# Output projection by seven block products instead of eight, in a hybrid pooling and attention block

## The chip, the cores and the metric

The kernel runs on one core of one Trainium2 chip. The metric is device microseconds of one execution; several executions are timed, and one more is recorded by the hardware profiler. TensorE is the matmul engine, VectorE and ScalarE do the elementwise work, GpSimd a part of it, and SyncE (SP) and ScalarE issue the DMA transfers.

## The reference

The block maps 1024 tokens of 1024 channels (with 16 meta tokens ahead of them). A normalised input is projected into branches; a pooling branch and an attention branch give `y_pool` and `y_attn` (512 channels each), and both are projected up, gated, merged and projected out:

```python
merged = (sigmoid(g_pool) * einsum('blc,cd->bld', y_pool, w_up_pool)
          + sigmoid(g_attn) * einsum('blc,cd->bld', y_attn, w_up_attn))
h = x + einsum('bld,de->ble', merged, w_out)          # 1024 x 1024 by 1024 x 1024
out = rmsnorm(h, final_norm_g)
```

Everything is float32. The change touches the last three lines.

## The kernel before

A float32 product is made of three matmuls of a reduced type: each operand is split into a high part (a copy, on ScalarE) and a low part (the difference, on VectorE or GpSimd), and high x high, high x low and low x high are summed in PSUM (`g_mm3`, `o_mm`). TensorE's instructions stand in the order of the program. The other engines' instructions and the DMA issues are put in order by a scheduler at compile time: each engine takes what its model holds ready, earlier lines of the program first; on the chip each engine then works its list off in that order.

The program ends in these stages. (1) Attention, with the projections of the gates between its steps; the gates are spilled to DRAM. (2) `pooled` for four groups, `attn_gate` and `attn_out` for four pairs of heads. `attn_out` loads the softmax denominators (`rc`), scales Y and splits it. (3) Sixteen up projections, `up(j, a)`: channel block j of 128, pooling (a = 0) or attention (a = 1). Each takes 24 matmuls of 512 columns; `up_weights` loads its weights (`rawu`, two buffers), splits them (`whu`, `wlu`) and reloads the gate (`rl`). In `up(j, 1)` the sum of both branches is split into `gh` (ScalarE) and `gl` (GpSimd). They stand in the order (0,0), (1,0), (2,0), (0,1), (3,0), (1,1) and so on. (4) `wo_chunk` loads the output weights in eight chunks through the same two buffers and splits them. (5) The output: eight tiles of 128 rows, two halves of 512 columns, 24 matmuls each; the last half is cut into two of 256 columns in two banks of PSUM. `out_tile` adds the residual, squares and sums, takes the power on GpSimd, scales and stores. The first three tiles are run in two passes over the weights' chunks.

The PSUM banks of (3) and (5) are taken in turn from two pools of three (`bank`). Tile pools hand out a fixed number of buffers per tag: 8 of tag "b" (gates and `rc`), 8 of tag "y", 13 of tag "g", and 16 of `hq`, which takes the place of the normalised input when the last input projection is done (`HX.close`).

Of the kernel before, what the change touches and what calls it, by code (L numbers as in the profile page):

```python
# [8 lines left out]
F32 = mybir.dt.float32  # L9
# [5 lines left out]
D = 1024  # L15
# [38 lines left out]
def tile_hybrid_block(ctx, tc, x, meta, norm_g, w_in, b_forget, pool_w, pool_scale,  # L54
# [76 lines left out]
    def w_chunk(col, **kw):  # L131
# [573 lines left out]
    def pool_mm(zp, g, plh, pll):  # L705
        yh = btile("yh", F32R, "y")
        yl = btile("yl", F32R, "y")
        for c0, c1 in HALVES:
            ps = bank()
            run(g_mm3(ps, [(pwh[:, g], pwl[:, g], plh[:, c0:c1], pll[:, c0:c1])]))  # L710
            nc.vector.scalar_tensor_tensor(zp[:, c0:c1], ps, psc[:, g:g + 1], zp[:, c0:c1], op0=ALU.mult, op1=ALU.mult)
            nc.scalar.activation(yh[:, c0:c1], zp[:, c0:c1], AF.Copy)
            yls.append(nc.gpsimd.tensor_tensor(yl[:, c0:c1], zp[:, c0:c1], r32(yh[:, c0:c1]), op=ALU.subtract))
        ypl[g] = (yh, yl)

    def attn_in(p):
# [2 lines left out]
        Y[p] = y  # L719

    def attn_gate(p, zs):
        ins = nc.gpsimd.tensor_tensor(Y[p], Y[p], zs, op=ALU.mult)
        if p > 1:
            after(ins, yls[-1])

    def attn_out(p):
        rc = btile("rc")
# [63 lines left out]
    def up(j, a, ws):  # L791
        y = (ypl, ya)[a]
        wh, wl, sg_ = ws
        after(nc.scalar.activation(sg_, sg_, AF.Sigmoid), evacs[-1])
        if a:
            gh = gp.tile([128, SEQ], F32R, name="gh", tag="g")
            gl = gp.tile([128, SEQ], F32R, name="gl", tag="g") if j < 5 else btile("gl", F32R)
            mg.append((gh, gl))
# [55 lines left out]
    run(left[3])  # L854
    attn_gate(2, za[2])
    HX.close()
    hq = ctx.enter_context(tc.tile_pool(name="hq", bufs=16, side="right", reuse_waits="tile"))
    attn_gate(3, za[3])
    second_up = up_weights(1, 0)

    wo = {}

    def wo_chunk(k):
        raw = wp.tile([128, D], F32, name="rawo", tag="raw")
        nc.sync.dma_start(raw, wout[:, k, :])
        hi = hq.tile([128, D], F32R, name="woh", tag="h")
        lo = hq.tile([128, D], F32R, name="wol", tag="h")
        nc.scalar.activation(hi, raw, AF.Copy)
        nc.vector.tensor_tensor(lo, raw, r32(hi), op=ALU.subtract)
        wo[k] = (hi, lo)  # L870

    up(0, 0, first_up)
    for p in range(4):
        attn_out(p)
    up(1, 0, second_up)
    for j in range(8):
        if j < 6:
            up(j + 2, 0, up_weights(j + 2, 0))
        up(j, 1, up_weights(j, 1))
        if j in (2, 3, 4, 5):  # L880
            wo_chunk(j - 2)
    for k in range(4, 8):
# [11 lines left out]
    def out_tile(i, parts):
        r = slice(i * 128, (i + 1) * 128)
        xr = btile("xr", F32, "y")
        sq = btile("sq", F32, "y")
        nc.sync.dma_start(xr, x2[r, :])
        ss = sm.tile([128, 4], F32, name="sso")
        tot = sm.tile([128, 1], F32, name="sst")  # L900
        for n, (ps, c0, c1) in enumerate(parts):
            if ps is None:
                ps = bank()
                o_mm(ps, i, c0, c1, range(KO))
            nc.vector.tensor_tensor(xr[:, c0:c1], ps[:, :c1 - c0], xr[:, c0:c1], op=ALU.add)
            nc.scalar.activation(sq[:, c0:c1], xr[:, c0:c1], AF.Square, scale=D ** -0.5, accum_out=ss[:, n:n + 1])
            if n == 0:
                nc.gpsimd.tensor_scalar(tot, ss[:, :1], EPS, None, op0=ALU.add)
            else:
                nc.gpsimd.tensor_tensor(tot, tot, ss[:, n:n + 1], op=ALU.add)  # L910
            nc.vector.tensor_tensor(xr[:, c0:c1], xr[:, c0:c1], fgb[:, c0:c1], op=ALU.mult)
        nc.gpsimd.tensor_tensor(tot, tot, epsp, op=ALU.pow)
        (a0, a1), (b0, b1) = HALVES
        nc.vector.tensor_scalar(sq[:, a0:a1], xr[:, a0:a1], tot, None, op0=ALU.mult)
        nc.sync.dma_start(o2[r, a0:a1], sq[:, a0:a1])
        nc.scalar.activation(sq[:, b0:b1], xr[:, b0:b1], AF.Copy, scale=tot)
        nc.scalar.dma_start(o2[r, b0:b1], sq[:, b0:b1])
# [12 lines left out]

_INS = ['x', 'meta_tokens', 'norm_g', 'w_in', 'b_forget', 'pool_w', 'pool_scale',
# [25 lines left out]
```

## Time and profile before

| | |
|---|---|
| median of 3 runs | 760.97 us (758.75 to 761.46) |
| profiled execution | 758.1 us |
| its span | 756.4 us |
| TensorE busy | 744.6 us, 98% |
| VectorE, ScalarE, GpSimd busy | 489.0, 370.4, 307.8 us |
| output stage (first to last matmul) | 660.6 to 750.1 us |

The span is what the profiler's rows cover; the execution's own time lies 1.7 us above it. Busy shares are over the whole span, so a stage has to be read in its own window. TensorE's rows are pipelined: each lasts longer than the distance to the next start, and the distance is what counts.

### The profile page before, as it was taken

The numbers are of one execution on the slowest core, as the hardware profiler recorded it, in microseconds if no ns is written. First come the engines' busy times: TensorE is split into PE (matmuls) and PEld (weight loads), VectorE is DVE, ScalarE is ACT, GpSimd is POOL, SyncE is SP. The second block draws the span as 40 slices with busy tenths as digits, with TensorE's granted clock in tenths as the row PEclk, the third lists the DMA queues.
The fourth block names the chain that finished last, engine by engine and source line by source line (L and its number), as shares of the span: only waits on it lengthen the run. The fifth ranks groups of instructions, "written<-read, shape, count | busy, mean of one in ns | idle before, by whom it ended". The sixth has DMA issues, their size and how long they took to land.

```text
span 756.4 us, 10583 instructions
## 1 busy us (share of the span) xinstructions
PE 744.6 (98%) x3746; PEld 633.6 (84%) x3746; DVE 489.0 (65%) x935; ACT 370.4 (49%) x708; POOL 307.8 (41%) x338
## 2 busy tenths in 40 slices
PE   8999999999999999999999999999999999999996
PEld 5997999998898898898988888888888788888885
DVE  4753667768779787698697766891566555534322
ACT  6662456446557555575565445531745553313112
POOL 4331336446416544544364354453573123213111
PEclk9999999999999999999999999999999999999999
DMA  9201132221221222221223322349447663523231
GB/s 312 71 20 38 29 94 75 72 85 50 78 61 45 80 63 70 83 60 50 74 66 105 98 74 78 91 149 339 136 168 208 236 196 102 177 84 132 91 112 55
DMA packets 78151, 79.54 MB, mean 105 GB/s; under 512 B 9857, under 2 KB 61057, under 8 KB 78098
## 3 DMA queue, kind: packets, MB, share of 16 engines
q1 hardware_dynamic: 73344, 63.65, 27.6%
q10 hardware_dynamic: 4754, 15.21, 5.9%
q8 instruction: 29, 0.48, 0.3%
q14 instruction: 24, 0.20, 0.1%
HBM read 57.68 MB, written 21.17 MB: 104 GB/s over the span
## 4 chain that ended last, share of the span: by engine, by line
PE 90%; DVE 3%; issue 1%; ACT 0%; POOLq 0%; POOL 0%; DVEq 0%; ACTq 0%
PE pj L139 67%; PE pj L891 12%; PE po L610 5%; PE ps L550 3%; PE ps L549 2%; PE pj L463 1%; PE pj L256 0%; DVE rl L803 0%; DVE yal L735 0%; DVE S L589 0%; DVE y L731 0%; DVE m L565 0%; ACT S L558 0%; DVE ka L243 0%; DVE xt L176 0%
## 5 line engine op out<-in xcount | busy, mean ns | idle before, releaser
L128 POOL TENSOR_TENSOR wlo<-raw,whi 128x256 fp32r<-128x256 f32 x148 | 121.8, 853 | 199.2 <-ACT whi L126 103.9
L139 PE MATMUL pj<-hh,whi 128*128 128x512 f32 (+4 forms) x768 | 178.9, 361 | 0.2 <-DVE V L262 0.2
L139 PE MATMUL pj<-hl,whi 128*128 128x512 f32 (+4 forms) x768 | 177.1, 359 | 0.0
L139 PE MATMUL pj<-hh,wlo 128*128 128x512 f32 (+4 forms) x768 | 174.7, 359 | 0.0
L139 PEld LDWEIGHTS pj<-hh,wlo 128*128 128x128 f32 x768 | 132.4, 188 | 18.2
L139 PEld LDWEIGHTS pj<-hh,whi 128*128 128x128 f32 x768 | 132.2, 189 | 18.0 <-PE pj L256 0.4
L139 PEld LDWEIGHTS pj<-hl,whi 128*128 128x128 f32 x768 | 131.6, 188 | 17.7
L594 DVE TENSOR_TENSOR pl<-S,ph 128x512 fp32r<-128x512 f32 (+4 forms) x112 | 86.8, 790 | 18.8 <-ACT ph L593 18.2
L602 POOL TENSOR_TENSOR acc<-acc,S 128x272 f32<-128x272 f32 (+4 forms) x80 | 76.4, 955 | 9.8 <-ACT S L590 4.7
L558 ACT ACTIVATE S<-ps,negc 128x400 f32<-128x400 f32 (+2 forms) x96 | 49.3, 515 | 45.1 <-DVE S L556 35.8
L590 ACT ACTIVATE S<-S 128x512 f32<-128x512 f32 (+4 forms) x112 | 49.5, 478 | 32.2 <-DVE S L589 32.0
L593 ACT ACTIVATE ph<-S 128x512 fp32r<-128x512 f32 (+4 forms) x112 | 52.2, 480 | 15.8 <-PE po L610 14.5
L565 DVE TENSOR_TENSOR m<-m,S 128x272 f32<-128x272 f32 (+4 forms) x80 | 41.4, 518 | 23.9 <-ACT S L558 22.2
L294 ACT ACTIVATE st<-pj 128x512 f32<-128x512 f32 x48 | 28.5, 594 | 50.9 <-PE pj L139 28.9
L589 DVE TENSOR_TENSOR S<-S,pt 128x512 f32<-128x512 f32 (+4 forms) x112 | 51.9, 498 | 0.8
L891 PE MATMUL pj<-woh,gl 128*128 128x512 f32 (+1 forms) x136 | 51.9, 382 | 0.0
L891 PE MATMUL pj<-wol,gh 128*128 128x512 f32 (+1 forms) x136 | 51.9, 381 | 0.0
L891 PE MATMUL pj<-woh,gh 128*128 128x512 f32 (+1 forms) x136 | 51.7, 380 | 0.0
L126 ACT ACTIVATE whi<-raw 128x1024 fp32r<-128x1024 f32 x37 | 39.1, 1056 | 25.1 <-PE pj L139 23.3
L807 POOL TENSOR_TENSOR gl<-rl,gh 128x512 fp32r<-128x512 f32 x16 | 22.3, 1396 | 70.9 <-ACT gh L806 70.9
L803 DVE TENSOR_TENSOR rl<-pj,rl 128x512 f32<-128x512 f32 x32 | 22.0, 689 | 31.3 <-PE pj L139 28.0
L556 DVE SCALAR_TENSOR_TENSOR S<-ps,negc,mask 128x128 f32<-128x128 f32 (+2 forms) x72 | 23.7, 330 | 23.0 <-PE ps L550 22.2
(165 smaller groups left out, 1107.4 us busy)
## 6 DMA issues: line engine op xcount, KB each, us to landing
raw<-in_w_in_dram SPq DMA_DIRECT2D x40, 512.0 KB, 3.9
sp_gp<-st SPq DMA_DIRECT2D x16, 256.0 KB, 2.0
sp_ga<-st SPq DMA_DIRECT2D x16, 256.0 KB, 2.0
rl<-sp_gp ACTq DMA_DIRECT2D x8, 512.0 KB, 4.7
rl<-sp_ga ACTq DMA_DIRECT2D x8, 512.0 KB, 4.3
rawo<-in_w_out_dram SPq DMA_DIRECT2D x8, 512.0 KB, 4.2
xr<-in_x_dram SPq DMA_DIRECT2D x8, 512.0 KB, 4.1
xt<-in_x_dram SPq DMA_DIRECT2D x7, 512.0 KB, 7.7
```

The source lines that it names most:

```text
L126: nc.scalar.activation(hi, raw, AF.Copy)
L128: nc.gpsimd.tensor_tensor(lo[:, k:k + 2], raw[:, k:k + 2], r32(hi[:, k:k + 2]), op=ALU.subtract)
L139: nc.tensor.matmul(ps, a, b, start=(i == 0), stop=(i == len(seq) - 1))
L558: nc.scalar.activation(s[:kb, f0:], ps[:kb, f0:], AF.Identity, bias=nb_)
L565: nc.vector.tensor_tensor(m[:kb, c0:], m[:kb, c0:], s[:kb, c0:], op=ALU.max)
L589: nc.vector.tensor_tensor(s[:kb, c0:], s[:kb, c0:], self.pm[:kb, c0:], op=ALU.subtract)
L590: exps.append(nc.scalar.activation(s[:kb, c0:], s[:kb, c0:], AF.Exp))
L593: nc.scalar.activation(ph[:kb, c0:], s[:kb, c0:], AF.Copy)
L594: dves.append(nc.vector.tensor_tensor(pl[:kb, c0:], s[:kb, c0:], r32(ph[:kb, c0:]), op=ALU.subtract))
L602: nc.gpsimd.tensor_tensor(acc[:kb, c0:], acc[:kb, c0:], s[:kb, c0:], op=ALU.add)
L610: nc.tensor.matmul(self.po[:, c0:], v, r[:kb, c0:], start=(b == 0 and i == 0), stop=(b == self.nb - 1 and i == 1))
L891: nc.tensor.matmul(ps[:, :c1 - c0], mg[k][a][:, r], wo[k][b][:, c0:c1], start=(k == 0 and n == 0), stop=(k == KO - 1 and n == 2))
```

## The change

The output product is made by a scheme of Strassen's kind (the form with seven products and fifteen additions): merged and w_out are cut into four blocks of 512 x 512 each. With A the merged activations and B the weights:

S1 = A21 + A22, S2 = S1 - A11, S3 = A11 - A21, S4 = A12 - S2; T1 = B12 - B11, T2 = B22 - T1, T3 = B22 - B12, and B21 - T2.
P1 = A11 B11, P6 = S2 T2, P2 = A12 B21, P7 = S3 T3, P5 = S1 T1, P4 = A22 (B21 - T2), P3 = S4 B22, run in this order.
The output blocks are C11 = P1 + P2, C12 = P1 + P6 + P5 + P3, C21 = P1 + P6 + P7 + P4, C22 = P1 + P6 + P7 + P5.

Each product has four tiles of 128 rows and 12 matmuls a tile, and its operands are split as before, one product ahead (`prep`), into two sets of buffers in turn. Sums that follow each other stay in PSUM (P2 on P1, P7 and P4 on P6, P3 on P5); the other additions go into the residual tiles `xr`. The additions of blocks run on GpSimd (S3, S4 and all T) and VectorE (S1, S2). The merged activations are kept unsplit (`G`), the weights are loaded whole into eight buffers. The pooling up projections 0 to 3 stand ahead of the first one of attention, and weights are asked for one projection ahead. GpSimd's two-input passes (`pool_tt`, `attn_gate`) are cut into pieces of 256 columns.

```diff
+    def pool_tt(out, x, y, op):
+        for c in range(0, out.shape[-1], 256):
+            ins = nc.gpsimd.tensor_tensor(out[:, c:c + 256], x[:, c:c + 256], y[:, c:c + 256], op=op)
+        return ins
...
-        for k in range(0, KO, 2):
-            nc.gpsimd.tensor_tensor(lo[:, k:k + 2], raw[:, k:k + 2], r32(hi[:, k:k + 2]), op=ALU.subtract)
+        pool_tt(flat(lo), flat(raw), flat(r32(hi)), ALU.subtract)
...
     def attn_gate(p, zs):
-        ins = nc.gpsimd.tensor_tensor(Y[p], Y[p], zs, op=ALU.mult)
...
+        for c in range(0, SEQ, 256):
+            ins = nc.gpsimd.tensor_tensor(Y[p][:, c:c + 256], Y[p][:, c:c + 256], zs[:, c:c + 256], op=ALU.mult)
...
             if a:
-                nc.vector.tensor_tensor(sg_[:, c0:c1], sg_[:, c0:c1], gt[j][:, c0:c1], op=ALU.add)
-                nc.scalar.activation(gh[:, c0:c1], sg_[:, c0:c1], AF.Copy)
-                nc.gpsimd.tensor_tensor(gl[:, c0:c1], sg_[:, c0:c1], r32(gh[:, c0:c1]), op=ALU.subtract)
+                nc.vector.tensor_tensor(G[j][:, c0:c1], sg_[:, c0:c1], gt[j][:, c0:c1], op=ALU.add)
...
+    hq = ctx.enter_context(tc.tile_pool(name="hq", bufs=8, side="right", reuse_waits="tile"))
...
+    def w_load(k):
+        W[k] = hq.tile([128, D], F32, name="W", tag="w")
+        nc.sync.dma_start(W[k], wout[:, k, :])
...
+    def split_op(op_, k, src):
+        h_ = pick(op_, k, 0)
+        nc.scalar.activation(h_, src, AF.Copy)
+        nc.vector.tensor_tensor(pick(op_, k, 1), src, r32(h_), op=ALU.subtract)
...
+    def t_first(k):
+        tt(Y3[k // 2][:, k % 2, :], side(W, k, "22"), side(W, k, "12"), ALU.subtract, nc.gpsimd)
+        tt(side(W, k, "12"), side(W, k, "12"), side(W, k, "11"), ALU.subtract, nc.gpsimd)
+    def t_second(k):
+        tt(side(W, k, "11"), side(W, k, "22"), side(W, k, "12"), ALU.subtract, nc.gpsimd)
+    def t_third(k):
+        tt(side(W, k, "21"), side(W, k, "21"), side(W, k, "11"), ALU.subtract, nc.gpsimd)
+    def s_first(k):
+        tt(X3[k // 2][:, k % 2, :], side(G, k, "11"), side(G, k, "21"), ALU.subtract, nc.gpsimd)
+    def s_second(k):
+        tt(side(G, k, "21"), side(G, k, "21"), side(G, k, "22"), ALU.add, nc.vector)
+        tt(side(G, k, "11"), side(G, k, "21"), side(G, k, "11"), ALU.subtract, nc.vector)
+    def s_third(k):
+        tt(side(G, k, "12"), side(G, k, "12"), side(G, k, "11"), ALU.subtract, nc.gpsimd)
...
+    steps = [(2, 0), (3, 0), (0, 1)]
+    for j in range(1, 8):
+        steps += [(j + 3, 0), (j, 1)] if j < 5 else [(j, 1)]
+    ws = {steps[0]: up_weights(*steps[0])}
     for p in range(4):
         attn_out(p)
     up(1, 0, second_up)
+    for n, s in enumerate(steps):
+        if n + 1 < len(steps):
+            ws[steps[n + 1]] = up_weights(*steps[n + 1])
+        up(*s, ws.pop(s))
+        if n < 8:
+            w_load((0, 4, 1, 5, 2, 6, 3, 7)[n])
+            if n % 2:
+                t_first(n // 2)
+        j, a = s
+        if a and j < 4:
+            s_first(j)
+        if s == (7, 0):
+            opA, opB = operand("y"), operand("y")
+        if a and j >= 4:
+            if j < 6:
+                for k in (2 * j - 8, 2 * j - 7):
+                    split_op(opA, k, side(G, k, "11"))
+                    split_op(opB, k, side(W, k, "11"))
+                    t_second(k)
+            if j == 5:
+                s_second(0)
+            if j > 4:
+                s_second(j - 4)
...
+    def prod(ps, A_, B_, i, start, c0=0, c1=512):
+        n = 0
+        for p, q in ((0, 0), (0, 1), (1, 0)):
+            for k in range(4):
+                nc.tensor.matmul(ps[:, c0:c1], pick(A_, k, p)[:, i * 128:(i + 1) * 128], pick(B_, k, q)[:, c0:c1],
+                                 start=start and n == 0, stop=n == 11, skip_group_check=True)
+                n += 1
...
+    def prep(n):
+        A_, B_ = operand("yh"[n % 2]), operand("yh"[n % 2])
+        sa, sb = srcs[n]
+        for k in range(4):
+            split_op(A_, k, side(G, k, sa) if sa else X3[k // 2][:, k % 2, :])
+            split_op(B_, k, side(W, k, sb) if sb else Y3[k // 2][:, k % 2, :])
+            if n == 2:
+                s_third(k)
+                t_third(k)
+        ops[n] = A_, B_
+    for n in range(7):
+        if n < 6:
+            prep(n + 1)
+        ps = bb_ if n in (1, 3, 5) else ba
+        for i in range(4):
+            if n == 6 and i == 3:
+                for c0, c1 in ((0, 256), (256, 512)):
+                    prod(ps[i], *ops[n], i, False, c0, c1)
+                    arrive(i, 512 + c0, ps[i][:, c0:c1])
+                    gain(i, 512 + c0, 512 + c1)
+                store(i, True)
+                continue
+            prod(ps[i], *ops[n], i, n in (0, 1, 4))
             if n == 0:
+                x1 = X1[i // 2][:, i % 2, :]
+                nc.scalar.activation(x1, ps[i], AF.Copy)
+                for r, c in ((i, 1), (i + 4, 1), (i + 4, 0)):
+                    tt(xr[r][:, T_[c]], xr[r][:, T_[c]], x1, ALU.add, nc.gpsimd)
+            elif n == 1:
+                nc.vector.tensor_tensor(xr[i][:, T_[1]], ps[i], xr[i][:, T_[1]], op=ALU.add)
+            elif n == 2:
+                arrive(i, 0, ps[i])
+                if i == 3:
+                    gain(i, 0, 512)
+            elif n == 3:
+                nc.vector.tensor_tensor(xr[i + 4][:, T_[1]], ps[i], xr[i + 4][:, T_[1]], op=ALU.add)
+            elif n == 4:
+                arrive(i + 4, 512, ps[i])
+            elif n == 5:
+                arrive(i + 4, 0, ps[i])
+                store(i + 4)
             else:
+                arrive(i, 512, ps[i])
+                store(i)
```

`arrive` adds a block from PSUM into `xr` (VectorE), squares it (ScalarE) and adds its sum on GpSimd; `gain` multiplies by the norm's gain; `store` takes the power on GpSimd, scales the row (one VectorE pass of 1024 columns with the gain; for the last row two halves, on VectorE and ScalarE) and stores it.

## Rows read from the trace of the kernel before

**Rows 1.** The page: busy time of each engine, and the granted clock in 40 slices.
```profile
PE 744.6 (98%) x3746; PEld 633.6 (84%) x3746; DVE 489.0 (65%) x935; ACT 370.4 (49%) x708; POOL 307.8 (41%) x338
...
PEclk9999999999999999999999999999999999999999
```
**Rows 2.** Windows: length, busy us (instructions) per engine, granted clock, DMA share, GB/s.
```profile
569.50:586.40 16.90, 16.90 (x74) 13.60 (x73) 12.96 (x13) 9.49 (x11) 4.73 (x2) 1.00 0.83 233
...
638.00:660.60 22.60, 22.60 (x98) 18.27 (x98) 12.37 (x17) 8.08 (x12) 7.96 (x6) 1.00 0.48 164
660.60:750.10 89.50, 89.48 (x409) 73.29 (x407) 32.29 (x47) 21.31 (x45) 17.84 (x25) 1.00 0.28 94
```
**Rows 3.** The chain that ended last: start us, us, what.
```profile
589.66 71.13 PE pj L139 x304
```
**Rows 4.** Timeline of TensorE in the output stage: start us, us, instructions.
```profile
660.62 0.39 PE L891 MATMUL pj<-woh,gh 128*128 128x512 f32 x1
...
744.24 0.28 PE L891 MATMUL pj<-woh,gh 128*128 128x256 f32 x1
...
749.80 0.28 PE L891 MATMUL pj<-woh,gl 128*128 128x256 f32 x1
```
**Rows 5.** Timeline at up(0,1): TensorE, its weight loads, VectorE; idle and releaser in brackets.
```profile
586.59 1.11 PE L139 MATMUL pj<-yah,whu 128*128 128x512 f32 x4
...
587.18 1.23 DVE L735 TENSOR_TENSOR yal<-y,yah 128x1024 fp32r<-128x1024 f32 x1
...
589.66 0.76 PEld L139 LDWEIGHTS pj<-yah,wlu 128*128 128x128 f32 x4 [1.01 <-DVE wlu L787]
...
590.70 1.10 PE L139 MATMUL pj<-yah,whu 128*128 128x512 f32 x4
```
**Rows 6.** Timeline of SP's queue, and GB/s in forty slices of 560 to 757 us.
```profile
571.28 4.95 SPq L730 DMA_DIRECT2D rc<-recs  x8
577.13 0.39 SPq L783 DMA_DIRECT2D rawu<-in_w_up_attn_dram  x1
...
642.69 0.65 SPq L898 DMA_DIRECT2D xr<-in_x_dram  x1
...
GB/s 53 0 169 250 297 107 375 152 348 137 226 98 298 107 106 106 114 307 210 120 42 222 60 0 0 56 162 208 218 0 210 3 109 104 36 180 0 106 0 106
```
**Rows 7.** Groups by line and shape, 560 to 757 us: busy us, mean ns, idle.
```profile
L806 ACT ACTIVATE gh<-rl 128x512 fp32r<-128x512 f32 x16 | 10.0, 630 | 25.3 <-DVE rl L805 25.3
L905 DVE TENSOR_TENSOR xr<-pj,xr 128x512 f32<-128x512 f32 x15 | 10.4, 691 | 34.4 <-PE pj L891 30.0 <-DMA out_dram<-sq 4.4
```
**Rows 8.** Single lines: duration ns min/median/max, first and last start, shapes.
```profile
L128 POOL TENSOR_TENSOR wlo<-raw,whi x148: 729/743/1731, 51.3 to 545.5; 128x256 fp32r<-128x256 f32 x148
L722 POOL TENSOR_TENSOR y<-y,rl x4: 2395/2634/3400, 546.2 to 571.4; 128x1024 f32<-128x1024 f32 x4
L807 POOL TENSOR_TENSOR gl<-rl,gh x16: 1286/1302/2093, 593.1 to 666.2; 128x512 fp32r<-128x512 f32 x16
L754 DVE SCALAR_TENSOR_TENSOR u<-s,u x4: 1226/1648/2203, 506.1 to 553.1; 128x1024 f32<-128x1024 f32 x4
L787 DVE TENSOR_TENSOR wlu<-rawu,whu x16: 681/682/1867, 555.6 to 650.3; 128x512 fp32r<-128x512 f32 x16
L803 DVE TENSOR_TENSOR rl<-pj,rl x32: 676/692/693, 573.3 to 662.0; 128x512 f32<-128x512 f32 x32
L805 DVE TENSOR_TENSOR rl<-rl x16: 678/691/1741, 591.6 to 663.2; 128x512 f32<-128x512 f32 x16
```
**Rows 9.** Timeline of VectorE and GpSimd where a 512-column pass meets 256-column pieces.
```profile
484.66 1.13 DVE L594 TENSOR_TENSOR pl<-S,ph 128x512 fp32r<-128x512 f32 x1
...
484.49 2.61 POOL L128 TENSOR_TENSOR wlo<-raw,whi 128x256 fp32r<-128x256 f32 x3
```
**Rows 10.** Timeline of the tail: the last addition and the last issue.
```profile
750.12 0.42 DVE L905 TENSOR_TENSOR xr<-pj,xr 128x256 f32<-128x256 f32 x1 [1.40 <-PE pj L891]
...
753.02 0.34 ACTq L917 DMA_DIRECT2D out_dram<-sq  x1
```

More of the change, by code (lines that the diff above doesn't have):

```diff
@@ L795, in up @@
         if a:
[L796 to L798 removed]
+            G[j] = gp.tile([128, SEQ], F32, name="G", tag="g")
         for c0, c1 in HALVES:
@@ L856, in tile_hybrid_block @@
     HX.close()
-    hq = ctx.enter_context(tc.tile_pool(name="hq", bufs=16, side="right", reuse_waits="tile"))
+    hq = ctx.enter_context(tc.tile_pool(name="hq", bufs=8, side="right", reuse_waits="tile"))
     attn_gate(3, za[3])
     second_up = up_weights(1, 0)
[L861 to L870, printed above, removed]
+    W = {}
@@ new lines, in tile_hybrid_block, with tt, operand @@
+    T_ = (slice(0, 512), slice(512, 1024))
+    def w_load(k):
+        W[k] = hq.tile([128, D], F32, name="W", tag="w")
+        nc.sync.dma_start(W[k], wout[:, k, :])
+    def tt(out, x, y, op, eng):
+        if eng is nc.gpsimd:
+            pool_tt(out, x, y, op)
+        else:
+            eng.tensor_tensor(out, x, y, op=op)
+    def operand(tag):
+        return [[(bp if tag == "y" else hq).tile([128, 2, 512], F32R, name="op" + tag, tag=tag, bufs=8) for _ in range(2)]
+                for _ in range(2)]
@@ new lines, in pick, with side @@
+    def pick(op_, k, n):
+        return op_[n][k // 2][:, k % 2, :]
+    def split_op(op_, k, src):
+        h_ = pick(op_, k, 0)
+        nc.scalar.activation(h_, src, AF.Copy)
+        nc.vector.tensor_tensor(pick(op_, k, 1), src, r32(h_), op=ALU.subtract)
+    X3 = [gp.tile([128, 2, 512], F32, name="X3", tag="g") for _ in range(2)]
+    Y3 = [gp.tile([128, 2, 512], F32, name="Y3", tag="g") for _ in range(2)]
+    def side(d, k, blk):
+        r, c = {"11": (0, 0), "12": (0, 1), "21": (1, 0), "22": (1, 1)}[blk]
+        return d[k + 4 * r][:, T_[c]] if d is W else d[k + 4 * c][:, T_[r]]
@@ L894, in out_tile @@
[L894 to L906, printed above, removed]
-            if n == 0:
-                nc.gpsimd.tensor_scalar(tot, ss[:, :1], EPS, None, op0=ALU.add)
-            else:
[L910 to L917, printed above, removed]
@@ new lines, in tile_hybrid_block @@
+    fgb = gp.tile([128, D], F32, name="fgb", tag="g")
+    nc.scalar.dma_start(fgb, bass.AP(tensor=final_g.tensor, offset=final_g.offset, ap=[[0, 128], [1, D]]))
+    xr = {}
+    for r in (0, 4, 1, 5, 2, 6, 3, 7):
+        xr[r] = btile("xr")
+        nc.sync.dma_start(xr[r], x2[r * 128:(r + 1) * 128, :])
+    bk = [pool.tile([128, 512], F32, name=n) for pool, n in
+          ((pj, "pj"), (pj, "pj"), (pj, "pj"), (psT, "pt"), (p8, "pj"), (p8, "pj"), (p8, "pj"), (psT, "pt"))]
+    ba, bb_ = bk[:4], bk[4:]
@@ new lines, in tile_hybrid_block, with gain @@
+    X1 = [wp.tile([128, 2, 512], F32, name="X1", tag="raw") for _ in range(2)]
+    sss, tots, cnts = {}, {}, {}
+    def prod(ps, A_, B_, i, start, c0=0, c1=512):
[5 more added lines that the diff above has]
+                n += 1
+    def gain(r, c0, c1):
+        nc.vector.tensor_tensor(xr[r][:, c0:c1], xr[r][:, c0:c1], fgb[:, c0:c1], op=ALU.mult)
@@ new lines, in arrive @@
+    def arrive(r, c0, ps):
+        w = ps.shape[-1]
+        part = xr[r][:, c0:c0 + w]
+        nc.vector.tensor_tensor(part, ps, part, op=ALU.add)
+        if r not in cnts:
+            sss[r] = sm.tile([128, 4], F32, name="sso", bufs=8)
+            tots[r] = sm.tile([128, 1], F32, name="sst", bufs=8)
+            cnts[r] = 0
+        n = cnts[r]
+        cnts[r] += 1
+        sq = stg.tile([128, 512], F32, name="sq", tag="st")
+        nc.scalar.activation(sq[:, :w], part, AF.Square, scale=D ** -0.5, accum_out=sss[r][:, n:n + 1])
+        if n == 0:
+            nc.gpsimd.tensor_scalar(tots[r], sss[r][:, :1], EPS, None, op0=ALU.add)
+        else:
+            nc.gpsimd.tensor_tensor(tots[r], tots[r], sss[r][:, n:n + 1], op=ALU.add)
@@ new lines, in store @@
+    def store(r, last=False):
+        o, t = wp.tile([128, D], F32, name="o", tag=("wh", "wl")[r % 2]), tots[r]
+        rr = slice(r * 128, (r + 1) * 128)
+        nc.gpsimd.tensor_tensor(t, t, epsp, op=ALU.pow)
+        (a0, a1), (b0, b1) = HALVES
+        if last:
+            nc.vector.tensor_scalar(o[:, a0:a1], xr[r][:, a0:a1], t, None, op0=ALU.mult)
+            nc.sync.dma_start(o2[rr, a0:a1], o[:, a0:a1])
+            nc.scalar.activation(o[:, b0:b1], xr[r][:, b0:b1], AF.Copy, scale=t)
+            nc.scalar.dma_start(o2[rr, b0:b1], o[:, b0:b1])
+        else:
+            nc.vector.scalar_tensor_tensor(o, xr[r], t, fgb, op0=ALU.mult, op1=ALU.mult)
+            nc.sync.dma_start(o2[rr, :], o)
```

38 lines of the change are left out of this document (9 added, 29 removed).

## The prediction

> **What bounds the kernel now.** I read the page's busy times first: TensorE is busy 98% of the span and its granted clock is at the top (the 2.4 GHz level) in all forty slices [rows 1]. So a saving counts only if it takes matmuls away, and a cost only if it makes TensorE wait. The windows then show where the change falls: the up projections from 569.5 us, the output projection from 660.6 to 750.1 us with TensorE busy 89.48 of 89.50 us [rows 2]. The chain of waits says the same: from 589.66 us it is matmuls back to back [rows 3]. The reader is to see that VectorE, ScalarE and GpSimd have room in the output stage before, so that nobody but TensorE sets its length; the question is whether that stays so.
>
> **What the change removes.** Output matmuls before: fifteen 512-column blocks of 24, so 360, and 48 of 256 columns in the last block. From the first start at 660.62 to the first narrow one at 744.24 us is 83.62 us for 360, 0.2323 us each; the 48 narrow ones fill 744.24 to 750.08, 0.122 us each [rows 4]. After: seven products of four row tiles of 12 are 336, of which the last tile is cut in two, so 324 wide and 24 narrow: 324 x 0.2323 + 24 x 0.122 = 78.2 us for 89.5 before. **Term 1: -11.3 us.**
>
> Before, up(0,1) waits for the attention rows. Its twelve first matmuls run from 586.59 to 590.70 us, 4.11 us for 12 x 0.2323 = 2.79; the weight loads name the last product of attn_out and wlu as releasers [rows 5]. With the pool projections 2 and 3 ahead of it, up(0,1) comes one projection later (24 x 0.2323 = 5.6 us, so at 592.2), while the last yal ends at 587.18 + 1.23 = 588.4. **Term 2: -1.3 us**, with 3.8 us of slack.
>
> **What it adds on the loading side.** The eight W loads (0.5 MB each) no longer wait for two shared buffers: their eight buffers come free with the last projection, near 569.5 us. The queue of SP there holds the eight rc loads (571.28 to 576.23), which attn_out waits for, and then the weights of the next projections at 577.13 [rows 6]. DMA is already at a share of 0.83 between 569.5 and 586.4 us [rows 2]. All eight W in front of rc would move 4.19 MB at the highest rate of a slice here, 375 GB/s [rows 6], so rc and the weights behind it would be 11.2 us late, 7.4 after the slack. None in front costs nothing. The rc loads stand ahead of W in the program and are ready when the last spill store has left, so I take few in front. **Term 3: +1.0 us** (0 to 7.4).
>
> **What it adds on VectorE and GpSimd.** The products take no plain operands; each needs eight halves of 512 columns split into high and low (ScalarE 0.63 us, VectorE 0.69 us each [rows 7, 8]). ScalarE has 8 x 0.63 = 5.0 us of this in a product of 48 x 0.2323 = 11.15 us, plus four copies or squares (2.5 us): hidden. VectorE has 8 x 0.69 = 5.5 us, plus four additions from PSUM at 0.69 [rows 7]: 8.3 of 11.15, hidden too, unless GpSimd is in the way. And it is: a VectorE pass with both inputs in SBUF takes 0.69 alone and up to 1.74 us while GpSimd runs (L805), whereas the pass with one input from PSUM never takes more than 0.693 (L803) [rows 8]. One such meeting with 256-column GpSimd pieces: the 512-column pass takes 1.13 us instead of its 0.68, between pieces that then take 0.87 on average instead of 0.743 [rows 8, 9]. So they take turns, and each turn costs VectorE 0.45 us. The pieces of 256 columns thus hold it less than the 512-column ones before (1.302 us, and L787 at up to 1.87 [rows 8]).
>
> GpSimd's new pieces: 32 in the up stage (t_first 16, s_first 8, t_second 8, for sixteen 1.302 us passes removed) and 40 from the first product on (24 additions of P1, 16 for s_third and t_third). The 40 take 40 x 0.743 = 30 us alone and some 40 x 1.2 = 48 taking turns, so GpSimd is there until product 3 or 4. In such a product VectorE needs 8 x 1.13 + 4 x 0.69 = 11.8 us, 0.65 more than TensorE: 0.65 x 3 to 5 products = 2.0 to 3.3 us if nothing is in reserve.
>
> The reserve is decided in the last four up projections, 4 x 5.57 = 22.3 us of TensorE. VectorE has there 4 x (4 x 0.69 + 0.68) = 13.8 us of the old work, eight splits at 0.68 for product 0 and six of the s_second additions at 0.69, together 23.3, and with t_second's eight turns up to 26.9. So it enters product 0 between 1.0 and 4.6 us late. In product 0 it has the last half's 1.4, s_second(3)'s 1.4 and eight splits at 1.13: 11.8. The low halves are first read by the fifth to eighth matmul of product 1, so 11.15 + 1.6 = 12.75 us is due: TensorE waits 0.1 to 3.7 us. All bounds: 0 (VectorE finds gaps earlier) to 3.7 + 3.3 = 7.0. What is late next is each following prep, since its buffers come free only with the product before. I take the lower middle, since the due time of 1.6 us is granted again at every product. **Term 4: +2.5 us** (0 to 7.0).
>
> The Trainium skill (GPSIMD Engine Reference, Engine selection) speaks against this change: it gives elementwise passes to VectorE and calls GpSimd about half as fast for two inputs. By the rows a 512-column pass costs VectorE 0.69 us if it does it itself, and 2 x 0.45 = 0.9 if GpSimd does it against a VectorE that is always at such a pass [rows 8, 9]. By the rule the 40 pieces would thus be 20 x 0.69 = 13.8 us on VectorE in place of at most 18, and the sum of term 4 at its upper end some 4 us smaller; by the rows the pieces that meet a PSUM pass or an idle VectorE are free, and the chosen value stands.
>
> GpSimd's own changes ahead of this (yl in 2 x 0.743 for 1.302, gates in 4 x 0.743 for 2.634 us [rows 8]) add 0.2 to 0.35 us each, under 3 us in all. What covers them is GpSimd's idle time: it is busy 4.73 of the 16.9 us from 569.5 on [rows 2]; without that cover up(0,0) would start up to 3 us later. The pieces of split_w keep their size. Nothing.
>
> **The tail.** Before, the last matmul is followed by addition, square, the sums and power on GpSimd, scaling and store, from 750.1 to 756.4 us, 6.3 us [rows 10]. After, the same chain, with two differences. Both halves of the last tile lie in one bank, so the second half's matmuls may wait until VectorE has read the first: 0 to 0.9 us (the 0.42 us read [rows 10] and the hops around it, doubled); I take 0.5. And row 2's store, a two-input pass of 1024 columns, 1.23 us alone (L754's shortest, [rows 8]), is ready at about the time of the last addition, since rows end 2.8 us apart and no longer 11: 0 to 1.8 us, I take 0.7. **Term 5: +1.2 us** (0 to 2.7). The Trainium skill (PSUM — Partial Sum Buffer, PSUM bank collisions raise a hardware error) wants accesses of two engines to one bank kept apart by a semaphore; no run here shows it, and by it the 0.5 is paid in full.
>
> **The sum.** -11.3 - 1.3 + 1.0 + 2.5 + 1.2 = -7.9 us. The profiled execution takes 758.1 us (span 756.4), so 750.2; the runs shown have their median 2.9 us above it at 760.97, which I carry along: **753.0 us**.
>
> **Rivals.**
> *VectorE becomes the bound.* Term 4 at its upper end, 7.0: -12.6 + 1.0 + 7.0 + 1.2 = -3.4, so 757.6 us. For it: VectorE's counted work is over TensorE's in the last four projections and in products 0 to 3. Against: VectorE was idle for 10.2 of the last 22.6 us of the up stage before [rows 2], and gaps earlier in the stage can take splits.
> *The W loads run ahead.* Term 3 at 7.4: -12.6 + 7.4 + 2.5 + 1.2 = -1.5, 759.5 us. For it: nothing but the order of issue holds them, and before, SP issued the first xr load at 642.69 us, well ahead of its use [rows 6]. Against: rc is ahead in the program.
> *Slower: GpSimd wins two turns for each of VectorE's.* Place: the splits of products 1 to 4. A split then takes about 1.87 us as L787's longest [rows 8]; 8 x 1.87 + 2.8 = 17.7, 6.6 us over the product, four times 26. -12.6 + 1.0 + 1.2 + 26 = +15.6, 776.6 us. It decides from the point where four products lose 12.6 us, a split of 1.44 us. For it: such long passes occur. Against: those rows met GpSimd passes of 512 columns and more, and the row with 256 shows 1.13.
>
> **How the numbers follow.** Forecast 0.66; VectorE the bound 0.14; W ahead 0.10; two turns for one 0.10. Half a per cent, 3.8 us, is about what this kernel's measurement can tell from no change: faster is below 757.2, slower above 764.8 us. The forecast with terms 3 to 5 between low and middling values reaches from 748.4 (terms 1 and 2 alone with almost nothing lost) to about 757; nearly all of it is faster. VectorE the bound falls on both sides of 757.2, mostly within; W ahead is within. Faster 0.68, same 0.22, slower 0.10. The range takes in the two middle rivals and leaves out the last and the ends: 748 to 760.
>
> **What would show it.** Right: the output stage in 78 to 82 us with the matmuls 0.232 apart; no weight load of up(0,1) waiting; split passes on VectorE of 1.1 us while GpSimd has pieces and 0.69 later; TensorE's waits, if any, at the starts of products 1 to 4, released by VectorE's low halves. Wrong: splits of 1.4 us and more; weight loads between 580 and 600 us waiting for a DMA of weights or for rc; a wait at each product's start up to the last; a tail over 9 us.

## The result, and the profile after

The changed kernel takes 761.45 us (median of 20 runs, 759.68 to 763.53), the kernel before 759.81 us in the same comparison: a ratio of 1.002 (95% interval 1.0011 to 1.0029). The forecast was 753.0 us, 0.989 of the runs shown then, with a range of 748 to 760; the change does not gain, and loses about one and a half microseconds. The profiled execution takes 763.1 us, its span is 760.9 us.

The page of the kernel after, the lines that answer to [rows 1]:
```profile
PE 738.3 (97%) x3686; PEld 628.7 (83%) x3686; DVE 534.0 (70%) x985; ACT 378.9 (50%) x737; POOL 353.4 (46%) x414
...
PEclk9999999999999999999999999999999999999996
```
The 60 matmuls that the change takes away are gone (3746 to 3686), and TensorE is busy 6.3 us less, in a span that is 4.5 us longer. So it waits more. Where it waits is read from windows that are cut at the same places of the program: the stage of the gates and pooled rows, the up projections, the output, the tail. First the kernel before (columns as in [rows 2]):
```profile
500.49:569.49 69.00, 69.00 (x301) 56.05 (x300) 35.67 (x32) 30.18 (x39) 35.35 (x27) 1.00 0.61 209
569.49:660.39 90.90, 90.14 (x385) 72.14 (x384) 54.69 (x72) 43.06 (x55) 23.70 (x16) 1.00 0.60 191
660.39:749.67 89.28, 89.28 (x408) 73.28 (x407) 32.50 (x47) 21.52 (x45) 17.84 (x25) 1.00 0.28 95
749.67:756.40 6.73, 0.41 (x4) 0.20 (x2) 1.34 (x3) 1.23 (x3) 0.93 (x2) 0.90 0.20 78
```
The same four windows of the kernel after, and two short ones, around the ends of TensorE's two long waits (it resumes at 559.29 and at 751.51 us):
```profile
501.96:574.64 72.68, 70.86 (x302) 57.13 (x300) 33.38 (x32) 30.09 (x39) 41.23 (x46) 0.98 0.62 212
574.64:666.87 92.23, 90.10 (x386) 71.88 (x384) 62.06 (x83) 36.02 (x47) 31.42 (x35) 1.00 0.65 211
666.87:753.81 86.94, 78.51 (x349) 64.53 (x347) 69.45 (x86) 37.21 (x82) 50.29 (x63) 0.96 0.16 62
753.81:760.90 7.09, 0.62 (x3) 0.33 (x2) 1.34 (x3) 1.23 (x3) 0.91 (x2) 0.50 0.20 74
...
557.00:564.00 7.00, 5.18 (x17) 3.77 (x16) 2.27 (x3) 4.82 (x7) 5.60 (x8) 0.76 0.67 222
...
752.00:755.00 3.00, 2.44 (x12) 2.14 (x11) 0.85 (x2) 0.07 (x2) 0.43 (x1) 0.50 0.41 168
```
Read the lengths against each other: 3.7 us lost before the up projections, 1.3 us in them, 2.3 us won in the output, 0.4 us lost in the tail, so 3.0 us lost. The other 1.5 us of the spans' difference lies before 500 us, where both programs do the same work: in this execution the granted clock is 0.50 from 47.6 to 51.0 us, where it is 1.00 in the kernel before. These windows are of one execution each; over all runs the medians lie only 1.6 us apart. In the output TensorE is busy 78.51 of 86.94 us where it had no gap before. Of the 8.43 us that are missing 7.79 are one wait. Timelines of the kernel after near the end, one engine at a time (start us, us, engine, line, operation, count, idle and releaser):
```profile
738.41 0.68 DVE L975 TENSOR_TENSOR xr<-pt,xr 128x512 f32<-128x512 f32 x1
740.85 1.28 DVE L1000 SCALAR_TENSOR_TENSOR o<-xr,sst,fgb 128x1024 f32<-128x1024 f32 x1 [1.75 <-POOL sst L992]
742.05 0.68 DVE L975 TENSOR_TENSOR xr<-pj,xr 128x512 f32<-128x512 f32 x1
744.48 1.28 DVE L1000 SCALAR_TENSOR_TENSOR o<-xr,sst,fgb 128x1024 f32<-128x1024 f32 x1 [1.75 <-POOL sst L992]
745.68 1.28 DVE L975 TENSOR_TENSOR xr<-pj,xr 128x512 f32<-128x512 f32 x2
748.11 1.28 DVE L1000 SCALAR_TENSOR_TENSOR o<-xr,sst,fgb 128x1024 f32<-128x1024 f32 x1 [1.15 <-POOL sst L992]
749.84 1.28 DVE L1000 SCALAR_TENSOR_TENSOR o<-xr,sst,fgb 128x1024 f32<-128x1024 f32 x1 [0.44 <-POOL sst L992]
751.04 0.41 DVE L975 TENSOR_TENSOR xr<-pt,xr 128x256 f32<-128x256 f32 x1
...
739.19 0.64 ACT L983 ACTIVATE sq<-xr 128x512 f32<-128x512 f32 x1 [2.91 <-DVE xr L975]
...
740.26 0.55 POOL L992 TENSOR_TENSOR sst<-sst,epsp 128x1 f32<-128x1 f32 x1
...
751.51 2.93 PE L965 MATMUL pt<-opy 128*128 128x256 f32 x12 [7.79 <-DVE xr L975]
```
VectorE's list goes add (L975), scale (L1000), add, scale. A scale waits for its own row's square on ScalarE and power on GpSimd, 1.75 us with VectorE standing still in the steady part, and the next row's addition stands behind it. From 738.41 to 742.05 us that is 3.64 us a row, where TensorE delivers a row every 2.73 us (a product takes 10.93 us for four). VectorE falls behind row by row. The last tile's second half shares a bank with its first, whose read stands at the end of this queue, at 751.04 us; TensorE, done with the first half at 743.7 us, waits 7.79 us for it, and its last twelve matmuls take 2.93 us at the lower clock level, where the twelve of the first half took 1.59.

The wait before the up projections, on ScalarE, GpSimd and TensorE:
```profile
551.37 7.17 ACTq L698 DMA_DIRECT2D rl<-sp_gp  x2
...
547.51 6.92 POOL L731 TENSOR_TENSOR y<-y,rl 128x256 f32<-128x256 f32 x7
554.38 3.80 POOL L120 TENSOR_TENSOR yl<-rl,yh 128x256 fp32r<-128x256 f32 x4
558.15 0.71 POOL L731 TENSOR_TENSOR y<-y,rl 128x256 f32<-128x256 f32 x1
...
558.64 0.60 ACT L301 ACTIVATE st<-pj 128x512 f32<-128x512 f32 x1 [10.02 <-POOL yl L120]
558.89 0.33 ACTq L698 DMA_DIRECT2D rl<-sp_gp  x1
...
554.07 2.02 PE L146 MATMUL pj<-hh,wlo 128*128 128x512 f32 x8
...
559.29 3.52 PE L146 MATMUL pj<-hh,whi 128*128 128x512 f32 x8 [1.82 <-ACT st L301]
```
The kernel before at the same place, where a gate is one pass:
```profile
546.25 5.75 POOL L722 TENSOR_TENSOR y<-y,rl 128x1024 f32<-128x1024 f32 x2
...
548.69 3.67 ACTq L691 DMA_DIRECT2D rl<-sp_gp  x2
```
There the second of two reload issues ends at 552.36 us, right behind the second gate, which ends at 552.00. After the change, of the eight pieces that two gates now are, GpSimd runs seven, then four pieces of yl, then the eighth. The second reload issue ends only at 558.54 us, right behind the last piece of yl, which ends at 558.18 and is the releaser that the row names. The eighth piece, which ends at 558.86, lets the third reload go at 558.89. So ScalarE stands at the second issue until the yl pieces are through, and with it stands the evacuation (L301, the pass that reads a PSUM bank out) whose bank TensorE needs. Which buffer each reload goes into the rows do not name; that the yl pieces free the second one because the last gate piece now comes behind them is argued. The wait itself is 1.82 us; the eight matmuls after it take 3.52 us where eight took 2.02 before, and their window shows the clock at 0.76.

In the up projections TensorE waits until 593.50 us, 1.67 us, for whu of up(3,0), the high part of its weights, and then 0.46 us for wlu, the low part. (The expectations below count the waits of the weight loads at the same places, 2.1 and 0.9 us.) VectorE, ScalarE and TensorE there:
```profile
589.07 0.69 DVE L810 TENSOR_TENSOR rl<-pj,rl 128x512 f32<-128x512 f32 x1 [1.89 <-PE pj L146]
589.68 1.22 DVE L740 TENSOR_TENSOR y<-y,rc 128x1024 f32<-128x1024 f32 x1
...
590.93 1.06 ACT L743 ACTIVATE yah<-y 128x1024 fp32r<-128x1024 f32 x1 [3.25 <-DVE y L740]
...
592.84 1.14 ACT L795 ACTIVATE whu<-rawu 128x512 fp32r<-128x512 f32 x2
...
593.50 1.20 PE L146 MATMUL pj<-yh,whu 128*128 128x512 f32 x4 [1.67 <-ACT whu L795]
```
An evacuation that waits for TensorE (L810) stands ahead of attn_out's pass on its rows y (L740), that pass ahead of yah, their high part, and yah ahead of the weight split.

The splits of the products, the answer to term 4 (duration ns min/median/max):
```profile
L889 DVE TENSOR_TENSOR opy<-G,opy x16: 679/740/1229, 646.1 to 727.5; 128x512 fp32r<-128x512 f32 x16
L889 DVE TENSOR_TENSOR oph<-Y,oph x4: 1215/1223/1295, 695.5 to 701.3; 128x512 fp32r<-128x512 f32 x4
```
A split that meets GpSimd takes 1.22 us, never 1.87. TensorE waits for one of them once, in product 3: 0.64 us behind the end of the matmul ahead, and 1.1 us by the distance of the starts.

### The profile page after: what moved, and what is told of

It reads as the page before. It is cut to its first block, busy times and chain, and to the rows that moved or that the text cites. A ratio compares the mean times of both kernels' runs of the same rounds, so it can differ in the third digit from the quotient of the medians.

```text
span 760.9 us, 10628 instructions
## 1 busy us (share of the span) xinstructions
PE 738.3 (97%) x3686; PEld 628.7 (83%) x3686; DVE 534.0 (70%) x985; ACT 378.9 (50%) x737; POOL 353.4 (46%) x414
## 3 DMA queue, kind: packets, MB, share of 16 engines
q10 hardware_dynamic: 3746, 13.38, 4.9%
## 5 line engine op out<-in xcount | busy, mean ns | idle before, releaser
L146 PE MATMUL pj<-hh,whi 128*128 128x512 f32 (+4 forms) x768 | 181.4, 365 | 2.0 <-ACT st L301 1.8
L146 PEld LDWEIGHTS pj<-hh,whi 128*128 128x128 f32 x768 | 133.9, 192 | 20.3 <-ACT st L301 2.2
L146 PEld LDWEIGHTS pj<-hl,whi 128*128 128x128 f32 x768 | 133.3, 191 | 17.8
L601 DVE TENSOR_TENSOR pl<-S,ph 128x512 fp32r<-128x512 f32 (+4 forms) x112 | 89.4, 812 | 18.1 <-ACT ph L600 17.4
L301 ACT ACTIVATE st<-pj 128x512 f32<-128x512 f32 x48 | 28.5, 594 | 54.8 <-PE pj L146 27.7
L810 DVE TENSOR_TENSOR rl<-pj,rl 128x512 f32<-128x512 f32 x32 | 22.0, 688 | 29.3 <-PE pj L146 26.8
L617 PE MATMUL po<-pl,V 128*128 128x512 f32 (+4 forms) x112 | 37.6, 336 | 0.1
L557 PE MATMUL ps<-ql,ka 128*128 128x512 f32 (+4 forms) x112 | 37.5, 334 | 0.0
L556 PE MATMUL ps<-qa,ka 128*128 128x512 f32 (+4 forms) x112 | 35.9, 321 | 0.5 <-ACT S L565 0.5
L617 PE MATMUL po<-ph,V 128*128 128x512 f32 (+4 forms) x112 | 36.3, 324 | 0.0
```

What stands on the lines that cost most here:

```text
L146: nc.tensor.matmul(ps, a, b, start=(i == 0), stop=(i == len(seq) - 1))
L557: nc.tensor.matmul(ps[:kb, c0:], ka[:, k0:k0 + kb], ql[:, q0 + c0:q0 + 512], start=False, stop=True)
L601: dves.append(nc.vector.tensor_tensor(pl[:kb, c0:], s[:kb, c0:], r32(ph[:kb, c0:]), op=ALU.subtract))
L617: nc.tensor.matmul(self.po[:, c0:], v, r[:kb, c0:], start=(b == 0 and i == 0), stop=(b == self.nb - 1 and i == 1))
```

## The experiments

Theory A: the wait at the end comes from VectorE's chain of stores. Rival B: it is the price of the shared bank. Theory C: the wait at 557 us comes from the pieces of the gates. Rival D: it only covers a wait that follows, and would be paid there. Ratios are to the kernel before in the same comparison; differences between kernels of different comparisons are taken from the ratios.

**late**: each row's store behind the next row's addition.
```diff
...
-                arrive(i, 512, ps[i])
-                store(i)
+                put_off(i, arrive(i, 512, ps[i]))    # store(previous row), its scale behind this row's addition
```


> The changed kernel with each row's store emitted one row later, so that VectorE adds the next row from PSUM before it scales the last one. Theory A (in the last two products VectorE's list is a chain of add, square, sum, power, scale per row, 3.64 us long for rows that TensorE makes every 2.75 us, and the last tile waits for its end): the 7.8 us wait ahead of the last half tile falls under 1 us, the half-speed clock behind it goes too, the time falls by 7 to 9 us, to 0.988 to 0.993 of the kernel before. Rival B (the wait is the price of the shared PSUM bank itself): most of the wait stays, the time falls by less than 2 us.

Measured: 751.48 us, ratio 0.9901 (0.9881 to 0.9920). TensorE's wait in the last tile (us in total, times, longest) is 0.9 us:
```profile
PE pt L965 <- DVE xr L975: 0.9, 1, 0.9
```
VectorE's timeline of this kernel:
```profile
735.90 0.69 DVE L975 TENSOR_TENSOR xr<-pj,xr 128x512 f32<-128x512 f32 x1 [0.68 <-PE pj L965]
736.51 1.28 DVE L1001 SCALAR_TENSOR_TENSOR o<-xr,sst,fgb 128x1024 f32<-128x1024 f32 x1
738.62 0.69 DVE L975 TENSOR_TENSOR xr<-pj,xr 128x512 f32<-128x512 f32 x1 [0.84 <-PE pj L965]
```
The additions now wait for TensorE and the scales for nobody. Between the ratios 1.0020 and 0.9901 lie 9 us, and they hung on the place of seven passes in VectorE's list. Theory A holds.

**uncut**: the last tile in one block, the stores as in the change.
```diff
-                for c0, c1 in ((0, 256), (256, 512)):
-                    prod(ps[i], *ops[n], i, False, c0, c1)
+                prod(ps[i], *ops[n], i, False)
```


> The changed kernel with the last tile in one block of 512 columns, so that no matmul waits for a read of its own bank; the stores as they are. Theory A (chain of stores on VectorE): TensorE's wait of 7.8 us is gone, but the last addition still stands at the end of VectorE's list, so that the end moves by only 2 to 4 us. Rival B (the shared bank): the time falls by 7 to 9 us.

Measured: 759.04 us, 0.9986 (0.9975 to 0.9998), 2.6 us under the changed kernel. TensorE's wait is gone altogether, and its last matmul starts 77.5 us after the stage's first, where it was 86.9; yet the addition behind the last scale stands where it stood, 83.9 us after that first matmul in both kernels:
```profile
748.39 1.28 DVE L1000 SCALAR_TENSOR_TENSOR o<-xr,sst,fgb 128x1024 f32<-128x1024 f32 x1 [0.44 <-POOL sst L992]
749.59 0.68 DVE L975 TENSOR_TENSOR xr<-pt,xr 128x512 f32<-128x512 f32 x1
```
The bank turned VectorE's lateness into a wait of TensorE; it was not its cause. Rival B falls, but for the 0.9 us of wait that late still shows.

**gate**: attn_gate in one pass of 1024 columns; **pieces**: the kernel before with the 256-column pieces alone.
```diff
-        for c in range(0, SEQ, 256):
-            ins = nc.gpsimd.tensor_tensor(Y[p][:, c:c + 256], Y[p][:, c:c + 256], zs[:, c:c + 256], op=ALU.mult)
...
+        ins = nc.gpsimd.tensor_tensor(Y[p], Y[p], zs, op=ALU.mult)
...
```


> The changed kernel with attn_gate as one GpSimd pass of 1024 columns again; everything else stays. Theory C (the last of eight gate pieces stands behind four yl pieces in GpSimd's list, so a gate buffer comes free late, ScalarE's reload issue waits for it 7 us, and the evacuation behind it holds up TensorE at 557 us, after which the clock is at half for seven matmuls): that wait and the slow stretch go, and the output ends 3 to 4 us earlier. Rival D (the time is set by the rc loads and attn_out that follow): the wait at 557 us goes, and the one at 591 us grows by as much, the time falls by less than 1 us.

> The kernel before with only GpSimd's pieces of 256 columns (pool_tt in split_w and yl, attn_gate), nothing else of the change. Theory C: the wait near 557 us shows here too and costs 2 to 4 us (1.003 to 1.005). As the prediction had it (covered by GpSimd's idle time): no wait, within 0.5 us (0.9995 to 1.0005).

Measured: gate 757.95 us, 0.9985 (0.9973 to 0.9997), 2.7 us under the changed kernel; pieces 762.16 us, 1.0038 (1.0022 to 1.0054), 2.8 us over the kernel before. In gate, where yl is still in pieces, the wait at 557 us is gone and the one at up(3,0) has not grown; in pieces, where there is no Strassen product, it is there and GpSimd's list shows the same seven, four and one:
```profile
546.74 6.90 POOL L729 TENSOR_TENSOR y<-y,rl 128x256 f32<-128x256 f32 x7
553.61 3.77 POOL L120 TENSOR_TENSOR yl<-rl,yh 128x256 fp32r<-128x256 f32 x4
557.34 0.72 POOL L729 TENSOR_TENSOR y<-y,rl 128x256 f32<-128x256 f32 x1
...
PE pj L144 <- ACT st L299: 2.8, 1, 2.8
```
That the cut of the gates makes this wait is shown, by taking the part away and by trying it alone, and rival D falls. One link of theory C does not hold as it was put: in both traces the reload goes when yl is done (557.38 us in pieces), and not with the last gate piece (558.06).

**late_gate**: both edits.

> Both repairs on the changed kernel: stores one row later, and attn_gate in one pass of 1024 columns. If the two causes are independent, the gains add: 0.990 x 0.9965, so 0.985 to 0.988 of the kernel before, some 9 to 11 us; the waits left for TensorE are those of up(3,0) near 586 us (2.1 and 0.9 us), of one product (1.1 us) and about 1 us in the last tile. If they cover the same time, it stays at 0.990.

Measured: 749.91 us, 0.9875 (0.9858 to 0.9892). The gains of late and gate add: their sum would be 0.9866, which lies in the interval. The waits left are those named. The next kernels start from this one.

**w30**: the weights of up(3,0) asked for ahead of the third attn_out; **w_behind**: each W load behind the last asked weights; **old_order**: the order of the up projections before; **attn_first** and **attn_ahead**: evacuations behind attn_out. The edit of old_order is not shown.
```diff
     for p in range(4):
+        if p == 2:
+            ws[steps[1]] = up_weights(*steps[1])          # w30
         attn_out(p)
...
-        nc.sync.dma_start(W[k], wout[:, k, :])
+        after(nc.sync.dma_start(W[k], wout[:, k, :]), asked[-1])          # w_behind
...
+            if (j, a) in ((1, 0), (2, 0)):          # attn_ahead; attn_first has (1, 0) alone
+                after(mul, yas[-1])
```


> Like late_gate, with the weights of up(3,0) asked for ahead of the third attn_out. Theory E (up(3,0), moved one projection forward, waits because ScalarE's list has its weight split behind yah of attn_out(2), which waits for VectorE): the waits of 2.1 and 0.9 us go, at most 1.3 us comes back at up(0,1), the time falls by 1 to 2.5 us. Rival F (the weights' load is late, crowded by the W loads): the waits stay within 0.3 us.

> Like late_gate, with each W load put behind the last weights asked for in the list of SP, so that no W load goes ahead of rc or of the weights of up(3,0). Theory E: the waits at up(3,0) stay within 0.3 us, the time within 0.5 us. Rival F (W loads crowd rc and the weights, term 3 of the prediction): the waits shrink by 1 us or more and the time falls with them.

> Like late_gate, with the up projections in the order of the kernel before (up(0,1) ahead of up(3,0)), and the splits for the first product one projection later, as its buffers demand. Theory E: the wait moves back to up(0,1) with 1.2 to 1.4 us, in place of 2.0 and 0.6 us net, so 0.5 to 1.5 us less, unless the later splits cost as much at the first product. The prediction's term 2 (the new order takes a wait of 1.3 us away): 1 to 1.5 us more.

Measured: w30 752.83 us, 0.9902 (0.9868 to 0.9936); w_behind 750.37 us, 0.9874 (0.9858 to 0.9891); old_order 755.17 us, 0.9943 (0.9928 to 0.9957). With w30 the waits at up(3,0) go and up(0,1) waits 1.9 us in their place: theory E had the chain right and the gain wrong, the wait is only handed on. w_behind does not change the time: the W loads, term 3, cost nothing that these runs show, and rival F falls. Theory E is not confirmed by it either: the wait at up(3,0) is one of 2.7 us, where it was 1.7 and 0.5, and ScalarE's row ahead of whu now waits 3.05 us for the reload of a gate. old_order is 5 us slower: TensorE waits three times at up(0,1) (1.7, 1.6 and 1.1 us) and three times more in the products, whose first splits come a projection later. In its profile the up projections take 2.5 us more than late_gate's and the products 0.9. So against theory E the new order, with the earlier splits that it allows, does help a kernel with this work on its lists; how much of it is the order alone stays open.

> Like late_gate, with VectorE's evacuation of up(1,0) put behind the last pass of attn_out in VectorE's list. Theory E2 (the waits of 2.1 and 0.9 us at up(3,0) come from VectorE's list, where evacuations that wait for TensorE stand ahead of attn_out's passes, so that ScalarE's weight split behind them is late): attn_out ends 3 to 5 us earlier, those waits go, the time falls by 1.5 to 3 us against late_gate, to 0.983 to 0.986. Rival (attn_out is late because rc lands late): the waits stay, the time stays within 0.5 us.

> Like late_gate, with VectorE's evacuations of both up(1,0) and up(2,0) behind the last pass of attn_out, so that no evacuation that waits for TensorE stands between attn_out's passes. Theory E2 (VectorE's list order makes attn_out late): attn_out's last low pass starts 4 us or more earlier, the waits of 2.1 and 0.9 us at up(3,0) go without another in their place, the time falls by 2 to 3.5 us against late_gate. Rival (rc lands late, and the list only shows it): VectorE waits for a DMA in their place, the waits shrink by less than 1 us.

Measured: attn_first 749.11 us, 0.9858 (0.9833 to 0.9883), waits as in late_gate. It missed its aim: VectorE now stood 2.6 us for the evacuation of up(2,0) ahead of attn_out's third pass. attn_ahead 749.81 us, 0.9861 (0.9837 to 0.9884): attn_out's last y pass starts at 585.21 us, 4.9 us earlier than in late_gate counted from the first up projection, and VectorE waits for no DMA there, so the rival of a late rc falls. One wait of 1.2 us is left, and ScalarE's rows name what holds whu now:
```profile
587.79 1.06 ACT L801 ACTIVATE rl<-rl 128x1024 f32<-128x1024 f32 x1 [2.62 <-DMA rl<-sp_gp]
588.75 0.61 ACT L793 ACTIVATE whu<-rawu 128x512 fp32r<-128x512 f32 x1
```
The up projections take 91.1 us in this profile, 92.3 in late_gate's. About half of the wait was VectorE's list; the rest stands behind the reload of a gate that lands late. By their times attn_ahead and late_gate cannot be told apart. How much of this rest is loads and how much ScalarE's list stays open.

**wide**: the additions of blocks in GpSimd passes of 512 columns; **on_vector**: the additions of P1 on VectorE.
```diff
-        if eng is nc.gpsimd:
-            pool_tt(out, x, y, op)
-        else:
-            eng.tensor_tensor(out, x, y, op=op)
+        eng.tensor_tensor(out, x, y, op=op)          # wide
...
-                    tt(xr[r][:, T_[c]], xr[r][:, T_[c]], x1, ALU.add, nc.gpsimd)
+                    tt(xr[r][:, T_[c]], xr[r][:, T_[c]], x1, ALU.add, nc.vector)          # on_vector
```


> Like late_gate, with the additions of blocks on GpSimd in single passes of 512 columns. Term 4's mechanism (VectorE and GpSimd take turns, and a split waits for the rest of a GpSimd pass): split passes that meet one take about 1.7 us in place of 1.2, GpSimd has 20 such passes from the first product on, so VectorE falls behind at products 1 to 3: waits of 3 to 8 us in sum in place of 1.1, the time 0.993 to 0.998. Rival (the width does not matter, since the passes take as long in sum): within 1 us of late_gate.

> Like late_gate, with the additions of P1 to three output blocks (24 GpSimd pieces) on VectorE, 12 passes of 512 columns. If a GpSimd piece that meets VectorE costs it 0.45 us and most of them meet it, the 24 pieces cost VectorE as much as the 12 passes at 0.69 (10.8 against 8.3 us): within 1 us of late_gate, with the wait moved from product 3 to product 1 or 2. If GpSimd's pieces are mostly free, VectorE gets some 8 us of work more in products 0 and 1 and TensorE waits 2 to 5 us more.

Measured: wide 755.48 us, 0.9942 (0.9920 to 0.9964), 5.6 us over late_gate. Groups by line in its products (busy us, mean ns):
```profile
L884 DVE TENSOR_TENSOR opy<-G,opy 128x512 fp32r<-128x512 f32 x12 | 12.2, 1054 | 2.7 <-ACT opy L883 2.7
...
L884 DVE TENSOR_TENSOR oph<-X,oph 128x512 fp32r<-128x512 f32 x4 | 6.4, 1644 | 0.0
```
The splits of the second row take 1.64 us where the pieces leave them at 1.22, and TensorE waits at the starts of products 1, 2 and 3, 4.7 us in all. The turns that VectorE and GpSimd take, and a price that grows with the width of the pass, are as term 4 had them. on_vector takes 748.66 us in five executions, 0.9849 (0.9825 to 0.9873): no difference from late_gate that the runs can tell, as expected where the pieces are mostly met. Its trace is of a sixth execution, of 1851.53 us, and says nothing of these five, so where the waits went stays open.

**late_gate_uncut** and **best** (late_gate with uncut and attn_ahead):

> Like late_gate, with the last tile uncut. The wait of about 0.9 us between its halves goes; the last chain has 512 columns in place of 256 (addition and square each 0.25 us longer) and starts 0.1 us earlier for the matmuls: 0 to 0.7 us gained, not to be told from late_gate by these runs unless the shared bank costs more than its wait.

> All four edits: stores one row later, attn_gate in one pass, evacuations behind attn_out, last tile uncut. If each does what its own run showed and E2 holds: 0.981 to 0.984 of the kernel before. If E2 falls: 0.985 as without it.

Measured: 748.84 us, 0.9849 (0.9827 to 0.9872), and 747.94 us, 0.9841 (0.9822 to 0.9859). Both are some 12 us under the kernel before, and their intervals overlap with each other and with late_gate's. The wait between the halves is gone.

## Why the prediction was wrong

The step that failed is the tail, term 5: it priced a row's store as one pass that meets one addition, +1.2 us, where the stores made VectorE's list a chain longer than TensorE's row and cost 9.3 us. Two smaller steps failed with it, term 2 and the pieces that were put at nothing. The sum was -7.9 us; by the windows it is +3.0, by the medians of all runs +1.6. Step by step, by the windows:

- **Term 1** (-11.3 us) held. The products are 10.93 us each, 0.2277 a matmul, where 0.2323 was carried over from before; why the distance is shorter no run shows. Without its waits the output would take 76.9 us: 86.94 less the wait of 7.79, 1.1 for the slow clock in the last half tile, and 1.1 at product 3. That is -12.4.
- **Term 2** (-1.3 us) failed: +1.3. The step took up(0,1)'s wait to vanish with 3.8 us of slack, and did not ask what up(3,0) waits for when it comes one projection earlier: its own weight split, behind attn_out on ScalarE. It is right only against old_order, whose later splits count with it.
- **Term 3** (+1.0 us): nothing by w_behind; the rival built on it falls.
- **Term 4** (+2.5 us, 0 to 7.0): 1.1 us. The mechanism (1.13 us forecast for a split that meets a piece, 1.22 found; wide for the width) was right, the size inside its bounds. Both rivals built on it, VectorE the bound and two turns for one, fall: VectorE did set the end, but by the order of its list and not by the amount of its work.
- **The pieces ahead of the products**, put at nothing, cost 3.7 us in the windows and 2.7 to 2.8 us by the times of gate and pieces. The step looked at GpSimd's idle time in a window from 569.5 us on and at the passes' durations, while the gates start between 546.2 and 571.4 us [rows 8]. It did not ask which reload waits for a buffer that the passes free and what stands behind it; there the pieces let other work in between, and two reload issues took 7.17 us in place of 3.67.
- **The tail** (+1.2 us, 0 to 2.7): 7.8 + 1.1 + 0.4 = 9.3 us, of which late gives back 9. The shared bank was seen and priced by one read, 0.42 us. What was missing is that seven stores stand in VectorE's list ahead of the following additions, in the steady part with 1.75 us of standing still each, so that rows cost 3.64 us against TensorE's 2.73. Most of it could be read ahead: in the kernel before a row's last addition, square, sum, power and scale stand in a row too and take 3.39 us, but rows 11.2 us apart hid them:

```profile
727.68 0.69 DVE L905 TENSOR_TENSOR xr<-pj,xr 128x512 f32<-128x512 f32 x1 [3.41 <-PE pj L891]
...
730.59 0.48 DVE L914 TENSOR_SCALAR sq<-xr,sst 128x512 f32<-128x512 f32 x1 [0.73 <-POOL sst L912]
```
None of the signs of being wrong named this place: the chain after the last matmul stayed at 7.1 us by the window, under the 9 us that were named, and the wait came between the halves of the last tile.

What the Trainium skill says of GpSimd (GPSIMD Engine Reference, Engine selection) is not contradicted by on_vector: the 12 passes are no worse on VectorE. Its rule on banks (PSUM — Partial Sum Buffer, PSUM bank collisions raise a hardware error) shows here as the wait of the second half for the first half's read, 0.9 us when VectorE is on time and 7.8 when it is not.

## What to carry to other kernels

When work is made shorter on the bounding engine, take the chain that follows each of its pieces and set its full length, standing still included, against the new distance between pieces; an engine that works off a list in order pays every wait of the chain. A store that waits for a result from two other engines belongs one row later in the list. Cutting a pass into pieces also cuts it open: look at what the scheduler can put before the last piece, and at who waits for the buffers that then come free later.

## What the runs showed of the hardware

A wait can cost TensorE more than its length. After 1.8 us of standing still at 557 us the granted clock in 557 to 564 us was 0.76, and eight matmuls of 512 columns took 3.52 us in place of 2.02; after 7.8 us the clock in 752 to 755 us was 0.50, which is 1.2 GHz of 2.4, and twelve of 256 columns took 2.93 us, where 48 took 5.84 us before. It need not: after the 1.67 us that end at 593.5 us the window from 593 to 600 us shows 1.00, and in late the same wait near 557 us, 1.61 us there, was followed by a clock of 1.00 and eight matmuls in 2.12 us. A split on VectorE that meets GpSimd takes 1.22 us with pieces of 256 columns and 1.64 with 512, for 0.68 alone.
